# One hybrid SSM and attention layer on Trainium2: the first SSM gate tile fetched into another pool, the last query block copied out at once, one branch output fetched earlier

## The chip, the cores and the metric

The kernel runs on one core of one Trainium2 chip. Time is the device time of one execution, in microseconds (us). Three runs of the kernel before gave 1013.17, 1014.81 and 1015.25 us, a median of 1014.81. A further execution was taken under the profiler: 1013.51 us, in which the span from the first to the last instruction is 1011.5 us. The remaining 2.0 us lie around the span.

Engines go by short names: PE is TensorE (matmuls), DVE is VectorE, ACT is ScalarE, POOL is GpSimd, SP is SyncE, which here issues nearly all of the DMAs.

## The reference, cut to what matters

One layer of a streaming encoder over a prompt of 1024 tokens and a sample of 32 new tokens with 512 cached ones. The model width is 1024, there are 8 heads of 64, and everything is float32.

```
h = rms_norm(x, g_norm) * (1 + scale) + shift
z = h @ w_in              # u, zs | q, k, v, za | indexer | two merge gates g_s, g_a
ys = ssm_scan(u ...)      # S5 state space model, then gelu, GLU, * silu(zs)
o  = dsa_attend(q, k, v)  # each 64-token chunk attends to the keys the indexer picks
ya = o * silu(za)
merged = sigmoid(g_s) * (ys @ w_ps) + sigmoid(g_a) * (ya @ w_pa)
x = x + gate * (merged @ w_o)
y = rms_norm(x, g_final)
```

Outputs are y for prompt and sample, the new keys and values, the indexer keys and the SSM states.

## The kernel before

**Products.** A float32 product is made of three PE matmuls. Each operand is split into a rounded high part and the low rest (names ending in H and L, or wh and wl for a weight), and high times high, low times high and high times low are added in PSUM (`mm3`, lines L271, L272, L273). A split costs a cast on ACT (L75) and a subtraction on DVE (L78), or for weights a cast (L259 or L263) and a subtraction on POOL (L264). The 1056 tokens are handled as three blocks of 256, 384 and 416 (`BW`), so the third block holds the end of the prompt and the 32 sample tokens.

**The weight stream Z.** Nearly all products with `w_in` and `w_ps` are jobs of a list, the `Stream` object `Z`. One job is 128 output columns: 8 (or 4) steps in depth for each of the three blocks. A job's block is built in a PSUM tile `pz`, of which there are two (`ps_z`). When its last matmul has been emitted, an evacuation `ev` reads the PSUM tile and frees it. `Z` does not emit this `ev` at once: it is put on a list (`Z.after`) and comes out once a given estimate of PE time (`Z.lag`, 1.0 in the attention part, or the job's own `lag`) has been emitted beyond it. PE, DVE and ACT run in the order in which the program emits their instructions, so the lag decides in front of which other DVE and ACT work an evacuation stands.

**Attention.** The heads go in four pairs p = 0 to 3. Each pair has a key job K, a value job V and a query job Q (`Heads`, K0 to Q3). For each row block of a pair the main loop emits scores on PE into `pss`, maxima and score tiles `Sm` on DVE (L1409), a scaling (L1425), transposes on PE into `pt` (L1496), the split of the transposed probabilities into PH (ACT, L1498) and PL (DVE, L1499), the product with V on PE into `pspo` (L1513, L1515), and the output `ob` and `ya` (L1518 to L1521). Between these steps `run(us)` lets `Z` emit some of its products as filler. A pair's output `ya` goes to memory (`yaD[p]`); pair 3 is split straight into `b3H`, `b3L`. The `ev` of a query job makes two ACT copies, one for each head (`qs`, L1332), two DVE subtractions (L1336), and for the third block two small DVE copies of the sample queries (`qsm`, L1338).

**The SSM product.** After Q3 the stream holds eight jobs m0 to m7, the product of the stored SSM output with `w_ps`. When m0 begins, `switch()` closes one pool and opens `fin` and `fb`, and `ps_branch` loads the stored SSM output into 24 tiles `b`, the operand parts of m0 to m7, block by block. Tiles `m` (`m1` in the code) hold the gate of each job: `m_load(f)` loads `thD[f]`, 528 KB, from a buffer in memory, and the job's `ev` on DVE (L1612, lag 0) multiplies it with the product in place. `m_load(0)` and `m_load(1)` are issued behind the 24 loads, `m_load(f + 2)` when job f begins.

**The attention product.** When attention ends, `yaD[0]` to `yaD[2]` are loaded from memory as `src` and `srs` (L1769, L1770) and split into `b` tiles. The three splits are emitted `SA`, `SA + SB` and `SA + 2 SB` estimated microseconds of stream time later (4, 5, 6). Then come eight jobs of the product with `w_pa` into `psm`, a PSUM set of four tiles. Each block goes through `evac_a`: DVE multiplies it with the attention gate `tgl` (L1799), adds a quarter of the m tile (L1800), ACT makes the high part `mH`, DVE the low part `mL` (L78). The tiles `tgl` come from memory (`thD[8 + f]`, L1811) into tag `stg`, a pool of two tiles; the first two of them are fetched far ahead, in the attention part. The last stage multiplies the merged tiles with `w_o`.

**SP** issues DMAs in program order. A DMA whose destination tile or semaphore is not free yet holds back those behind it.

Of the kernel before, what the change touches and what calls it, by code (L numbers as in the profile page):

```python
# [7 lines left out]
F32 = mybir.dt.float32  # L8
F32R = mybir.dt.float32r
# [7 lines left out]
T, TS, D = 1024, 32, 1024  # L17
NT = T + TS
# [22 lines left out]
KA, LA = 5.0, 1.0  # L41
RE = 2.9
LAG, RS, MS, RM, RB = 4.5, 4.6, 0.008, 14.0, 1
FA, FF, SA, SB = ((1.0, 2.4), (1.1, 2.4), (1.1, 1.4), (1.5, 1.5)), 0.08, 4.0, 1.0
YR = 3.9, 2.0, 2.0, 8.0, 3.0
MR, ML, YS, YW, HI, HG, JO, SF = (), 1, 10, 15, 0, 0, 8, (2, 2, 2, 1)
C_U, C_ZS, C_Q, C_K, C_V, C_ZA, C_QI, C_KI, C_GM = 0, 512, 1024, 1536, 2048, 2560, 3072, 3584, 3656
# [16 lines left out]
def body(nc, tc, I, O, dbg=None):  # L64
# [3 lines left out]
    te, ve, se, ge, sp = nc.tensor, nc.vector, nc.scalar, nc.gpsimd, nc.sync  # L68

    def f32(ap):  # L70
        return ap.bitcast(F32)
# [10 lines left out]
    stg = ctx.enter_context(tc.tile_pool(name="stg", bufs=2))  # L82
# [226 lines left out]
    class Later:  # L309
        def __init__(self, eng, todo):  # L310
            self.eng, self.todo = eng, todo
# [159 lines left out]
    for k in range(7):  # L471
        n = 1 << k
# [208 lines left out]
    wcol = lambda c, n=128: w_in[:, c:c + n]  # L681
# [89 lines left out]
    for t in START.split():  # L771
# [6 lines left out]
        else:  # L778
            n = t.rstrip("0123456789")
# [418 lines left out]
    for k in range(9):  # L1198
        n = 128 if k < 8 else 32
# [50 lines left out]
    yaD = [dram.tile([128, NT], F32, name=f"yaD{q}") for q in range(4)]  # L1250
# [8 lines left out]
    def cp(eng):  # L1259
        return se.copy if eng is se else eng.tensor_copy  # L1260
# [45 lines left out]
    class Heads:  # L1306

        def __init__(self, p, heng, eng):
            self.eng, self.V2, self.heng_v = eng, [None, None], ve if p == 0 else ge
            self.p, self.cs = p, slice(128 * p, 128 * p + 128)  # L1310
            self.kH, self.kL, self.qs = [None, None], [None, None], [None, None]
            self.ready, self.want = False, []

            def kbegin():
                self.kf = zfp.tile([128, NT], F32, name="zf", bufs=2)
                return lambda n, ps: cp(eng)(self.kf[:, ns(n)], ps)

            def vbegin():
                self.vf = zfp.tile([128, NT], F32, name="zf", bufs=2)
                return lambda n, ps: cp(eng)(self.vf[:, ns(n)], ps)  # L1320

            def qbegin():
                self.qs = [ap_.tile([128, T], F32R, name=f"qs{e}", bufs=1 + e) for e in range(2)]
                self.qsm = ap_.tile([128, 2, TS], F32, name="qsm", bufs=2)
                ge.memset(self.qsm, 0.0)

                def ev(n, ps):
                    w = min(BW[n], T - B0[n])
                    c = slice(B0[n], B0[n] + w)
                    for e in range(2):  # L1330
                        r = slice(64 * e, 64 * e + 64)
                        se.copy(self.qs[e][r, c], ps[r, 0:w])  # L1332
                    for e in range(2):
                        r, o = slice(64 * e, 64 * e + 64), slice(64 - 64 * e, 128 - 64 * e)
                        q_ = self.qs[e]
                        ve.tensor_sub(q_[o, c], ps[r, 0:w], f32(q_[r, c]))  # L1336
                        if n == 2:
                            ve.tensor_copy(self.qsm[r, e], ps[r, w:BW[2]])  # L1338
                return ev

            job = lambda n, c0, b, end: Job(f"{n}{p}", wcol(c0 + 128 * p), b, end, heng=heng, leng=ge)
            self.kjob, self.vjob = (job("K", C_K, kbegin, lambda: self.kside()),
                                    job("V", C_V, vbegin, lambda: self.vside()))
            self.qjob = job("Q", C_Q, qbegin, None)
# [239 lines left out]
    m1, PB = [], []  # L1584

    def ps_branch():
        for h in range(2):
            PB.append({})
        for n in range(2, -1, -1):
            for q in range(4):  # L1590
                for h in range(2):
                    PB[h][q, n] = late["fb"].tile([128, BW[n]], F32R, name=f"b{h}{q}{n}")
        for n in range(3):
            for q in range(4):
                for h in range(2):
                    sp.dma_start(f32(PB[h][q, n]), ysD[h][q][:, ns(n)])
        for f in range(2):
            m_load(f)

    def m_load(f):  # L1600
        if f < 8:
            m1.append(late["fin"].tile([128, NT], F32, name="m1", tag="mm", bufs=8))
            sp.dma_start(m1[f], thD[f])

    def psjob(f):
        def begin():
            if not f:
                switch()
            m_load(f + 2)

            def ev(n, ps):
                ve.scalar_tensor_tensor(m1[f][:, ns(n)], m1[f][:, ns(n)], 1.0, ps, op0=ALU.add, op1=ALU.mult)  # L1612
            return ev
        return Job(f"m{f}", I["w_ps"].rearrange("o d e -> (o d) e")[:, 128 * f:128 * f + 128], begin, kt=4, lag=0,
                   heng=se, leng=ge, rhs=lambda n, k: (PB[0][k, n], PB[1][k, n]))
# [77 lines left out]
    seq, first, half, end = [], {}, {}, {}  # L1693
# [7 lines left out]
    late = {}  # L1701

    def switch():
        st.close()
        late["fin"] = ctx.enter_context(tc.tile_pool(name="fin", bufs=1, reuse_waits="tile"))
        late["fb"] = stB.enter_context(tc.tile_pool(name="fb", bufs=1, reuse_waits="tile"))
        ps_branch()
    stB = ExitStack()
    for k in range(len(seq) + 3):
        it = at(k)  # L1710
        if k in first:
            p, begin = first[k]
            k0 = k
            if p:
                Z.until(f"Q{p}")
            if p == 3:
                b3H, b3L = (zfp.tile([128, NT], F32R, name=n, tag="zf", bufs=2) for n in ("b3H", "b3L"))
            else:
                Z.upto(f"V{p + 1}")
            begin()  # L1720
        if it:
            e_ = max(it.e, 0) if it.e >= 0 or p == 3 else 1
        f = FA[p][e_] + FF * (it.i + 1 if it else 5)
        if not k:
            run(RE)
        if it:
            it.scores()
        if k in half and p < 3:
            HD[p + 1].want.append(0)
            HD[p + 1].heads()  # L1730
            Z.upto(f"K{p + 2}" if p < 2 else "m7")
        if p and k == k0 + 2:
            HD[p].want.append(1)
            HD[p].heads()
        if it:
            it.maxima()
        if at(k - 1):
            at(k - 1).norm(0)
        run(f * 0.4)
        Z.turns(2)  # L1740
        if at(k - 3):
            at(k - 3).out()
        if k - 3 in end and end[k - 3][0] < 3:
            end[k - 3][1]()
            HD[p].values(1)
        if k + 3 in end and p < 3:
            Z.until(f"v{p + 1}")
            HD[p + 1].values(0)
        run(f * 0.3)
        if at(k - 2):  # L1750
            at(k - 2).turn()
        if at(k - 1):
            at(k - 1).norm(1)
        if it:
            it.exps()
        run(f * 0.3)
# [4 lines left out]
    wo = ctx.enter_context(tc.tile_pool(name="wo", bufs=1, side="right", reuse_waits="tile"))  # L1761
# [2 lines left out]
    Z.load(len(Z.jobs) - 1)  # L1764
    raw_a = wload(w_pa[:, 0:128], 4, 128)
    for q in range(3):
        src = f32(wo.tile([128, 2, 512], F32R, name="src", tag=("o16", "o17", "o07")[q]).rearrange("p a b -> p (a b)"))
        sms = wo.tile([128, TS], F32, name=f"srs{q}")
        sp.dma_start(src, yaD[q][:, 0:T])  # L1769
        sp.dma_start(sms, yaD[q][:, T:NT])  # L1770
        h_, l_ = (mp.tile([128, NT], F32R, name=f"b{h}{q}", tag="b" + "0123"[2 * q + h] if q < 2 else f"b{4 + h}")
                  for h in range(2))
        aH.append(h_)
        aL.append(l_)

        def parts(h_=h_, l_=l_, src=src, sms=sms):
            split(h_[:, 0:T], l_[:, 0:T], src, se, ve)
            split(h_[:, T:NT], l_[:, T:NT], sms, se, ve)
        Z.after(SA + q * SB, parts)
# [12 lines left out]
    mL = []  # L1792
    ps_phase()
    def evac_a(f, c, tg, ps):
        if len(mL) == f:
            mL.append(late["fin"].tile([128, NT], F32R, name="mL", tag="mm", bufs=8) if f else
                      fl_.tile([128, NT], F32R, name="mL0"))
        m2 = stg.tile([128, GM], F32, name="m2", tag="sth")[:, :c.stop - c.start]
        ve.scalar_tensor_tensor(m2, tg, 1.0, ps, op0=ALU.add, op1=ALU.mult)  # L1799
        ve.scalar_tensor_tensor(m2, m1[f][:, c], 0.25, m2, op0=ALU.mult, op1=ALU.add)  # L1800
        split(mH[f][:, c], mL[f][:, c], m2, se, ve)
        if c.stop == NT:
            ge.tensor_copy(mS[:, f, 0:32], mH[f][:, T:NT])
            ge.tensor_copy(mS[:, f, 32:64], mL[f][:, T:NT])
# [72 lines left out]
    for rows in ((0, 1, 2), (8,), (3,), (4,), (5,), (6,), (LAST,)):  # L1877
        xts = {}
        for hcol in range(2):
            for i in rows:  # L1880
                n = 128 if i < 8 else 32
# [67 lines left out]
```

## Time and profile before

| | before |
|---|---|
| times of three runs | 1013.17, 1014.81, 1015.25 us |
| the profiled execution's own time | 1013.51 us |
| its span | 1011.5 us |
| DVE busy | 763.3 us (75%) |
| ACT busy | 524.6 us (52%) |
| POOL busy | 234.6 us (23%) |
| mean granted TensorE clock | 0.991 |
| DMA traffic | 124.24 MB, mean 123 GB/s |

A row of the timeline gives the start in us, the duration in us, the engine, the source line, the operation, the tiles as output<-input, the shape and the number of instructions merged into the row. What stands in brackets is the idle time of the engine ahead of the row and what ended it; `issue` is time in which the engine waited for nothing that the profile can name. SPq rows are DMA issues: the duration is that of the issue, not of the transfer. A row of the windows view gives the stretch, its length, the busy time and count of PE, PEld, DVE, ACT and POOL, the granted clock of PE (1.00 is full speed), the busy share of the DMA engines and GB/s. Matmuls are pipelined: one of 416 columns is shown 0.35 us long, while the next one starts 0.19 us after it.

### The profile page before, as it was taken

What the parts mean: (1) busy time and instruction counts of PE and PEld (TensorE: products, weight loads), DVE (VectorE), ACT (ScalarE), POOL (GpSimd) and SP (SyncE); (2) the same over time, 40 slices, a digit from 0 to 9 for tenths busy, and PEclk for the clock granted to TensorE, in tenths of its full rate; (3) what the DMA queues carried; (4) which work ended last, traced back from release to release, by engine and by line L of the source; (5) the groups of instructions that cost most, each with busy time, mean ns of one, the idle gap of its engine ahead of it and who ended that gap; (6) DMA issues with size and microseconds to landing.
All of it is one profiled execution on the core that took longest, in us unless ns stands there. A gap on an engine that the chain in (4) does not pass through costs nothing.

```text
span 1011.5 us, 16910 instructions
## 1 busy us (share of the span) xinstructions
PE 968.2 (96%) x6034; PEld 904.1 (89%) x6034; DVE 763.3 (75%) x1747; ACT 524.6 (52%) x1126; POOL 234.6 (23%) x443
## 2 busy tenths in 40 slices
PE   5999999999999999999999989999998999999997
PEld 2789999999998898999999979899897989898786
DVE  4669979994776878889999976577577785885543
ACT  3642234433555656858896365565575564443111
POOL 3202400000000024343322743233222222430000
PEclk9999999999999999999999999999999999999999
DMA  9923425437484222333323422231329403552311
GB/s 315 289 66 101 133 70 140 113 95 203 164 256 151 64 63 64 105 83 98 118 74 114 141 87 64 85 106 55 107 66 332 136 22 109 182 188 105 126 63 62
DMA packets 134400, 124.24 MB, mean 123 GB/s; under 512 B 20401, under 2 KB 115077, under 8 KB 134317
## 3 DMA queue, kind: packets, MB, share of 16 engines
q1 hardware_dynamic: 133376, 122.62, 39.3%
q8 instruction: 47, 0.77, 0.3%
q10 hardware_dynamic: 780, 0.52, 0.2%
q14 instruction: 37, 0.30, 0.1%
q0 software_dynamic: 160, 0.03, 0.0%
HBM read 87.74 MB, written 34.83 MB: 121 GB/s over the span
## 4 chain that ended last, share of the span: by engine, by line
PE 50%; DVE 14%; ACT 10%; issue 4%; DMA 1%; POOL 0%; SPq 0%; POOLq 0%; ACTq 0%; DVEq 0%
PE pz L271 8%; PE pz L272 7%; PE pz L273 7%; ACT junkb L1567 7%; PE pss L1403 3%; PE pt L1496 3%; DVE junk L1569 3%; PE psm L1918 3%; PE psm L1919 3%; PE psm L1920 3%; PE pspo L1515 2%; PE pspo L1513 2%; PE psm L272 1%; PE psm L273 1%; PE psm L271 1%
## 5 line engine op out<-in xcount | busy, mean ns | idle before, releaser
L271 PE MATMUL pz<-hH,wh 128*128 128x384 f32 (+4 forms) x744 | 254.5, 342 | 2.4 <-ACT tg L713 2.0
L272 PE MATMUL pz<-hL,wh 128*128 128x384 f32 (+4 forms) x744 | 246.2, 331 | 0.0
L273 PE MATMUL pz<-hH,wl 128*128 128x384 f32 (+4 forms) x744 | 246.0, 331 | 0.0
L264 POOL TENSOR_TENSOR wl<-raw,wh 128x256 fp32r<-128x256 f32 (+1 forms) x180 | 134.7, 776 | 126.5 <-ACT wh L259 116.0
L271 PEld LDWEIGHTS pz<-hH,wh 128*128 128x128 f32 (+1 forms) x744 | 140.4, 189 | 7.5 <-ACT tg L713 2.3
L272 PEld LDWEIGHTS pz<-hL,wh 128*128 128x128 f32 (+1 forms) x744 | 139.9, 188 | 1.8
L273 PEld LDWEIGHTS pz<-hH,wl 128*128 128x128 f32 (+1 forms) x744 | 139.6, 188 | 1.4
L1567 ACT ACTIVATE junkb<-sco,thr 128x768 bf16<-128x768 f32 (+3 forms) x128 | 96.7, 756 | 31.0 <-DVE thr L1643 20.1
L1569 DVE TENSOR_SCALAR_CACHE_REDUCE junk<-sco,thr 128x1024 bf16<-128x1024 f32 (+2 forms) x96 | 105.5, 1098 | 2.2
L271 PE MATMUL pss<-hH,wh 128*128 128x256 f32 (+2 forms) x304 | 97.6, 321 | 0.1
L272 PE MATMUL pss<-hL,wh 128*128 128x256 f32 (+2 forms) x304 | 95.7, 315 | 0.0
L273 PE MATMUL pss<-hH,wl 128*128 128x256 f32 (+2 forms) x304 | 95.4, 314 | 0.0
L263 POOL CAST wh<-raw 128x256 fp32r<-128x256 f32 x88 | 38.0, 471 | 180.9 <-PE pz L272 109.6
L1498 ACT CAST PH<-pt 128x512 fp32r<-128x512 f32 (+2 forms) x96 | 43.0, 482 | 41.5 <-PE pt L1496 37.4
L1499 DVE TENSOR_TENSOR PL<-pt,PH 128x512 fp32r<-128x512 f32 (+2 forms) x96 | 50.4, 551 | 14.6 <-ACT PH L1498 13.7
L271 PEld LDWEIGHTS pss<-hH,wh 128*128 128x128 f32 x304 | 58.6, 193 | 2.6 <-issue 1.6
L272 PEld LDWEIGHTS pss<-hL,wh 128*128 128x128 f32 x304 | 58.1, 191 | 0.3 <-DVE hL L78 0.2
L1236 DVE SCALAR_TENSOR_TENSOR sco<-rl,wi,sco 128x384 f32<-128x384 f32 (+6 forms) x49 | 46.9, 963 | 15.2 <-ACT rl L1231 14.1
L273 PEld LDWEIGHTS pss<-hH,wl 128*128 128x128 f32 x304 | 58.1, 191 | 0.0
L1231 ACT ACTIVATE rl<-pss 128x384 f32<-128x384 f32 (+6 forms) x56 | 40.9, 738 | 28.6 <-PE pss L1229 23.1
L1416 ACT ACTIVATE Sm<-Sm,mx 128x128 f32<-128x128 f32 (+8 forms) x68 | 52.7, 775 | 0.8 <-DVE mx L1409 0.8
L1920 PE MATMUL psm<-o,mL 128*128 128x512 f32 (+1 forms) x136 | 51.8, 381 | 0.0
(401 smaller groups left out, 2174.9 us busy)
## 6 DMA issues: line engine op xcount, KB each, us to landing
raw<-in_w_in SPq DMA_DIRECT2D x44, 512.0 KB
thD<-tg SPq DMA_DIRECT2D x16, 528.0 KB
wm<-in_w_mod SPq DMA_DIRECT2D x8, 1024.0 KB
tgl<-thD SPq DMA_DIRECT2D x8, 528.0 KB
m<-thD SPq DMA_DIRECT2D x8, 528.0 KB
rraw<-in_w_mod SPq DMA_DIRECT2D x4, 1024.0 KB
kd<-kd SPq DMA_DIRECT2D x32, 128.0 KB
xo<-in_x_prompt SPq DMA_DIRECT2D x8, 512.0 KB
```

Source lines behind the costliest of these rows:

```text
L264: leng.tensor_sub(wl[:, c], raw[:, c], f32(wh[:, c]))
L271: te.matmul(ps, wh, xh, start=first, stop=False)
L272: te.matmul(ps, wh, xl, start=False, stop=False)
L273: te.matmul(ps, wl, xh, start=False, stop=last)
L1231: se.activation(rl[:m, :nk].rearrange("p (b c) -> p b c", c=w_), pv, AF.Relu)
L1236: ve.scalar_tensor_tensor(sco[i][:m, :nk], rl[:m, :nk], w, sco[i][:m, :nk], op0=ALU.mult, op1=ALU.add)
L1416: se.activation(P, P, AF.Exp, scale=-1.0, bias=self.mx, accum_out=self.rs)
L1498: se.copy(PH[:, b0:b1_, oc], src)
L1499: ve.tensor_sub(PL[:, b0:b1_, oc], src, f32(PH[:, b0:b1_, oc]))
L1567: se.activation(junkb[:m, :nk], x[:m], AF.Sign, bias=t, accum_out=cnt[:m, k:k + 1])
L1569: ve.tensor_scalar(junk[:m, :nk], x[:m], t, None, op0=ALU.is_lt, op1=ALU.add, accum_out=cnt[:m, k:k + 1])
L1920: te.matmul(ps, ml, wh, start=False, stop=last)
```

## The change

Three edits, made together. Line numbers from about L1341 on are shifted by 1 to 12 in the changed kernel.

1. The job Q3 gets `lag=0`, so that each of its blocks is copied out as soon as its last matmul is emitted.
2. `m_load(0)` leaves `ps_branch` and moves to the middle of pair 2, into a tile of tag `stg`. That is the place and the tile in which the first `tgl` was fetched; the first `tgl` now goes where the second was, and the second `tgl` is fetched when a tile of the pair becomes free, in the `w_pa` stage. The `m` and `mL` tiles get fixed tags `mm0` to `mm7` in place of one tag with eight buffers.
3. `yaD[0]`, stored since the end of pair 0, is loaded as one tile `y0` of 528 KB (tag `mm7`) when job m2 begins, during pair 3. The reload of q = 0 as `src` and `srs` at the end of attention goes; its split reads `y0`. The three splits are emitted at 1.0, 3.5 and 6.0 (`SA, SB = 1.0, 2.5`).

```
-..., 4.0, 1.0
+..., 1.0, 2.5                                   # the last two are SA, SB
...
-            job = lambda n, c0, b, end: Job(f"{n}{p}", wcol(c0 + 128 * p), b, end, heng=heng, leng=ge)
+            job = lambda n, c0, b, end: Job(f"{n}{p}", wcol(c0 + 128 * p), b, end, heng=heng, leng=ge,
+                                            lag=0 if f"{n}{p}" == "Q3" else None)
...
-        for f in range(2):
-            m_load(f)
+        m_load(1)

     def m_load(f):
         if f < 8:
-            m1.append(late["fin"].tile([128, NT], F32, name="m1", tag="mm", bufs=8))
+            m1.append(late["fin"].tile([128, NT], F32, name="m1", tag=f"mm{f - 1}") if f else
+                      stg.tile([128, NT], F32, name="m1", tag="stg"))
             sp.dma_start(m1[f], thD[f])
+
+    def y0_load():
+        late["y0"] = late["fin"].tile([128, NT], F32, name="y0", tag="mm7")
+        sp.dma_start(late["y0"], yaD[0])
...
             m_load(f + 2)
+            if f == 2:
+                y0_load()
...
             Z.upto(f"K{p + 2}" if p < 2 else "m7")
+            if p == 2:
+                m_load(0)
...
     for q in range(3):
-        src = ...
-        sms = ...
-        sp.dma_start(src, yaD[q][:, 0:T])
-        sp.dma_start(sms, yaD[q][:, T:NT])
+        if q:
+            ...
+        else:
+            src, sms = late["y0"][:, 0:T], late["y0"][:, T:NT]
...
-            mL.append(late["fin"].tile([128, NT], F32R, name="mL", tag="mm", bufs=8) if f else
+            mL.append(late["fin"].tile([128, NT], F32R, name="mL", tag=f"mm{f - 2 if f > 1 else 7}") if f else
```

**DVE around the third block of Q3.** This is the program's order on DVE, in the last row blocks of pair 2. `qs_8318` and `qs_8319` (`qs_8320` and `qs_8321` in the changed kernel) are the query tiles of pair 3's two heads, `PL` the probabilities' low part, `Sm` a score tile, `m_8713` the gate tile of m0. Before:

```order
L1521 TENSOR_TENSOR ya<-ob,ya 64x256
L1499 TENSOR_TENSOR PL<-pt,PH 128x4x128
L1499 TENSOR_TENSOR PL<-pt,PH 128x128
L1409 ISA Sm,mx<-pss,mb_3324 128x512
L1409 ISA mx 128x1
L1409 ISA Sm,mx<-pss,mb_3324,mx 128x512
L1409 ISA mx 128x1
L1421 RECIPROCAL rs<-rs 128x1
L1425 TENSOR_SCALAR Sm<-Sm,rs 128x896
L1336 TENSOR_TENSOR qs_8318<-pz,qs_8318 64x384
L1338 COPY qsm<-pz 64x32
L1336 TENSOR_TENSOR qs_8319<-pz,qs_8319 64x384
```

In the changed kernel the same place reads:

```order
L1522 TENSOR_TENSOR ya<-ob,ya 64x256
L1336 TENSOR_TENSOR qs_8320<-pz,qs_8320 64x384
L1338 COPY qsm<-pz 64x32
L1336 TENSOR_TENSOR qs_8321<-pz,qs_8321 64x384
L1338 COPY qsm<-pz 64x32
L1500 TENSOR_TENSOR PL<-pt,PH 128x4x128
L1500 TENSOR_TENSOR PL<-pt,PH 128x128
L1410 ISA Sm,mx<-pss,mb_3324 128x512
```

The four instructions that read the PSUM tile `pz` of Q3's third block moved ahead of two `PL`, two score steps and the scaling. PE's own order up to the end of Q3 is the same in both.

**ACT at the end of attention.** These are the casts that make the high parts for the `w_pa` stage; the `b` with the lowest number is q = 0. `wh` is a weight cast of the `w_pa` stage. Before:

```order
L75 CAST b3H<-qs_8843 64x512
L75 CAST b_9794<-src 128x1024
L75 CAST b_9794<-srs_9791 128x32
L259 CAST wh<-raw 128x512
L75 CAST b_9800<-src 128x1024
L75 CAST b_9800<-srs_9797 128x32
L75 CAST b_9806<-src 128x1024
L75 CAST b_9806<-srs_9803 128x32
```

In the changed kernel:

```order
L75 CAST b3H<-qs_8843 64x512
L75 CAST b_9792<-y_9059 128x1024
L75 CAST b_9792<-y_9059 128x32
L75 CAST b_9798<-src 128x1024
L75 CAST b_9798<-srs_9795 128x32
L259 CAST wh<-raw 128x512
L75 CAST b_9804<-src 128x1024
L75 CAST b_9804<-srs_9801 128x32
```

The first cast reads `y0` (here `y_9059`) in place of a fresh `src`, and the weight cast moved from behind the first split to behind the second.

**SP at the same place.** These are its rows from the last weight load ahead of the reloads; what stands in brackets is what a row waits for, by the names of the semaphores: `DMAHW` for the end of an earlier DMA, else the engine. `thD_215`, `thD_216` and `thD_217` are the attention gates of f = 0, 1 and 2. Before:

```order
L250 DMA raw<-in_w_pa 128x4x128 [waits DMAHW3_49,DMAHW7_49,Activation_49,Pool_49]
L1769 DMA src<-yaD_4200 128x1024 [waits PE_49]
L1770 DMA srs_9791<-yaD_4200 128x32
L1769 DMA src<-yaD_4201 128x1024
L1770 DMA srs_9797<-yaD_4201 128x32
L1769 DMA src<-yaD_4202 128x1024 [waits DMAHW4_49]
L1770 DMA srs_9803<-yaD_4202 128x32 [waits DMAHW5_49]
```

In the changed kernel, on to the first gate load that is issued there:

```order
L250 DMA raw<-in_w_pa 128x4x128 [waits DMAHW3_49,Activation_49,Pool_49]
L1779 DMA src<-yaD_4201 128x1024 [waits DMAHW0_49,PE_49]
L1780 DMA srs_9795<-yaD_4201 128x32
L1779 DMA src<-yaD_4202 128x1024
L1780 DMA srs_9801<-yaD_4202 128x32
L1833 DMA gate_10411<-growD 128x1024 [waits DMAHW4_49]
L1833 DMA gate_10412<-growD 32x1024 [waits DMAHW5_49]
L1836 DMA gf<-in_g_final 128x1024 [waits DMAHW6_49]
L250 DMA raw<-in_w_pa 128x4x128 [waits DMAHW7_49,Activation_49,Pool_49]
L1823 DMA tgl<-thD_216 128x1056 [waits DMAHW0_49,DVE_49]
```

Two loads fewer stand there, so that q = 1 and q = 2 each move up one place, and the gate of f = 1 is loaded there, after a wait for DVE, where before the first gate load of this stretch was that of f = 2 (`thD_217`).

More of the change, by code (lines that the diff above doesn't have):

```diff
@@ L43 @@
 LAG, RS, MS, RM, RB = 4.5, 4.6, 0.008, 14.0, 1
-FA, FF, SA, SB = ((1.0, 2.4), (1.1, 2.4), (1.1, 1.4), (1.5, 1.5)), 0.08, 4.0, 1.0
+FA, FF, SA, SB = ((1.0, 2.4), (1.1, 2.4), (1.1, 1.4), (1.5, 1.5)), 0.08, 1.0, 2.5
 YR = 3.9, 2.0, 2.0, 8.0, 3.0
@@ L1766, in body @@
     for q in range(3):
-        src = f32(wo.tile([128, 2, 512], F32R, name="src", tag=("o16", "o17", "o07")[q]).rearrange("p a b -> p (a b)"))
-        sms = wo.tile([128, TS], F32, name=f"srs{q}")
-        sp.dma_start(src, yaD[q][:, 0:T])
-        sp.dma_start(sms, yaD[q][:, T:NT])
+        if q:
+            src = f32(wo.tile([128, 2, 512], F32R, name="src", tag=("", "o17", "o07")[q]).rearrange("p a b -> p (a b)"))
+            sms = wo.tile([128, TS], F32, name=f"srs{q}")
+            sp.dma_start(src, yaD[q][:, 0:T])
+            sp.dma_start(sms, yaD[q][:, T:NT])
+        else:
+            src, sms = late["y0"][:, 0:T], late["y0"][:, T:NT]
         h_, l_ = (mp.tile([128, NT], F32R, name=f"b{h}{q}", tag="b" + "0123"[2 * q + h] if q < 2 else f"b{4 + h}")
```

## The prediction

> **What bounds the kernel now.** I read the page's shares of busy time first, then PE's waits, then windows around the places that the change touches. A row of the waits view gives the idle us that ended at that instruction, how often, and the longest.
>
> ```profile
> PE 968.2 (96%) x6034; PEld 904.1 (89%) x6034; DVE 763.3 (75%) x1747; ACT 524.6 (52%) x1126; POOL 234.6 (23%) x443
> ...
> PE pz L271 <- issue: 3.8, 1, 3.8
> PE psm L271 <- ACT b L75: 1.2, 3, 0.6
> ...
> 770.00:780.00 10.00, 7.71 (x40) 6.73 (x41) 5.13 (x15) 2.44 (x6) 1.78 (x5) 0.83 1.04 404
> 856.00:868.00 12.00, 10.72 (x62) 9.34 (x61) 5.94 (x12) 4.12 (x7) 1.71 (x4) 1.00 0.88 277
> ```
>
> PE is busy 96% of the span, so a change pays only where PE idles or runs at a lower clock. The change touches two such places: one single idle of 3.8 us at 770, with the granted clock of that window down to 0.83, and short waits for the casts of `b` at 856 to 868, 1.28 us by the window (12.00 less 10.72). No PE instruction is added or removed, so everything below is waits and clock.
>
> **Edit 1, Q3 copied out at once.** These are the rows around the long idle: PE, DVE, ACT.
>
> ```profile
> 765.24 0.35 PE L273 MATMUL pz<-hH,wl 128*128 128x416 f32 x1
> 768.19 0.28 PE L273 MATMUL pz<-b,wl 128*128 128x256 f32 x1
> 772.29 0.66 PE L271 MATMUL pz<-b,wh 128*128 128x384 f32 x1 [3.82 <-issue]
> ...
> 766.07 1.16 DVE L1521 TENSOR_TENSOR ya<-ob,ya 64x256 f32<-64x256 f32 x1
> 767.26 0.89 DVE L1499 TENSOR_TENSOR PL<-pt,PH 128x512 fp32r<-128x512 f32 x2
> 770.66 0.55 DVE L1336 TENSOR_TENSOR qs<-pz,qs 64x384 fp32r<-64x384 f32 x1
> 771.23 0.18 DVE L1338 COPY qsm<-pz 64x32 f32<-64x32 f32 x1
> 771.43 0.56 DVE L1336 TENSOR_TENSOR qs<-pz,qs 64x384 fp32r<-64x384 f32 x1
> 772.00 0.20 DVE L1338 COPY qsm<-pz 64x32 f32<-64x32 f32 x1
> ...
> 765.07 0.37 ACT L1518 COPY ob<-pspo 64x256 f32<-64x256 f32 x1 [1.37 <-PE pspo L1515]
> 769.12 0.96 ACT L1332 CAST qs<-pz 64x384 fp32r<-64x384 f32 x2
> ```
>
> The profile calls the idle "issue", but the time fits a PSUM wait. `pz` has two tiles; the second block of m0 takes the one that held Q3's third block, finished by PE at 765.59. Its last reader, the second `qsm` copy, ends at 772.20, and PE starts at 772.29. In the changed order these four readers stand right behind `ya`, which ends at 767.23. ACT is free at 765.44, so its two casts (0.96) are through by about 766.6 and hold nothing up. The four take 0.55 + 0.18 + 0.56 + 0.20 = 1.49, with gaps about 1.55: the tile is free at 768.8, and PE, done with the first block at 768.47, goes on at about 768.9. Idle 0.4 in place of 3.82: **3.4 us**.
>
> The idle also costs clock. The windows below are stretches at half clock; the two PE rows are other idles.
>
> ```profile
> 771.69:775.10 3.41, 2.81 (x11) 2.74 (x12) 0.49 (x2) 0.62 (x2) 0.00 (x0) 0.50 1.06 401
> 457.66:461.07 3.41, 3.41 (x10) 3.27 (x11) 3.27 (x9) 2.65 (x7) 0.00 (x0) 0.50 0.79 235
> ...
> 457.60 0.69 PE L271 MATMUL pz<-hH,wh 128*128 128x416 f32 x1 [1.96 <-ACT tg L713]
> 716.66 1.09 PE L1496 MATMUL pt<-idf,Sm 128*128 128x128 f32 x8 [1.21 <-ACT Sm L1423]
> ```
>
> Half clock came after an idle of 1.96, not after one of 1.21, so 0.4 should not bring it. In the first window PE worked 2.81 us at half speed, which is 1.40 us of work done late: **1.4 us** more. The stretch starts on a grid of 3.41 us, so other executions may have lost 0.7 to 1.7 here. [...]
>
> What is late next? The two `PL`, the scores and the scaling now run 1.5 us later, and PE runs ahead by 4.8.
>
> ```profile
> 776.33 0.42 DVE L1612 SCALAR_TENSOR_TENSOR m<-m,pz 128x256 f32<-128x256 f32 x1 [4.13 <-DMA m<-thD]
> 778.43 0.88 PE L1515 MATMUL pspo<-PL,V 128*128 128x256 f32 x6
> 779.14 0.35 PE L271 MATMUL pz<-b,wh 128*128 128x416 f32 x1
> ...
> 770.07 0.32 SPq L1596 DMA_DIRECT2D b<-ysLD  x1
> GB/s 0 89 290 265 124 260 244 266 299 211 294 276 172 328 332 315 357 361 399 398 394 412 406 391 425 414 413 414 383 339 374 356 271 265 321 425 401 328 36 234
> ```
>
> DVE: 4.13 us before m0's first gate product went to waiting for `m`, the tile that **edit 2** now loads during pair 2; without this wait DVE has room for the 1.5. By summing durations `PL` for the products at 778.43 is ready near 773.5, and PE comes there at 778.43 − 4.8 = 773.6: no margin, so 0 to 0.5 of new wait, taken as 0. Transfers: the last `b` left at 770.07 with its seven predecessors in flight, since each DMA here waits for the end of the one eight before it. That is at most 8 x 0.21 MB = 1.7 MB, and the row of GB/s (slices of 0.875 us from 755) shows about 0.4 MB a us: estimated landings from 771.1 to 774.3. PE wants the first pair of that block at 779.14 − 4.8 = 774.3 and the last 1.7 later, so they are in time by 1.7 or more. If they weren't, at most the 3.4 and 1.4 would be cut by the lateness. The moved `m_load(0)` stands on SP where a load of the same size stood, so it costs nothing there; behind the 24 `b` loads one load fewer is queued.
>
> **Edit 3, q = 0 fetched ahead.** The rows of SP, ACT and PE at the passage from attention to the `w_pa` product:
>
> ```profile
> 855.53 0.50 SPq L1769 DMA_DIRECT2D src<-yaD  x1
> ...
> 859.75 1.05 ACT L75 CAST b<-src 128x1024 fp32r<-128x1024 f32 x1 [4.34 <-DMA src<-yaD]
> 862.93 1.05 ACT L75 CAST b<-src 128x1024 fp32r<-128x1024 f32 x1 [0.85 <-DMA src<-yaD]
> 864.64 1.05 ACT L75 CAST b<-src 128x1024 fp32r<-128x1024 f32 x1 [0.54 <-DMA src<-yaD]
> ...
> 859.91 0.35 PE L273 MATMUL pz<-b,wl 128*128 128x416 f32 x1
> 864.03 0.75 PE L271 MATMUL psm<-b,wh 128*128 128x256 f32 x3 [0.44 <-ACT b L75]
> 868.40 0.34 PE L271 MATMUL psm<-b3H,wh 128*128 128x384 f32 x1
> 874.21 0.34 PE L271 MATMUL psm<-b3H,wh 128*128 128x384 f32 x1
> ```
>
> Three loads of 0.53 MB, the first issued at 855.53, land at about 859.7, 862.9 and 864.6; PE's last earlier work ends at about 860.1 (859.91 and the 0.19 until the next could start), then it follows the casts. One job of the stage takes 874.21 − 868.40 = 5.81, so 1.45 for each q. From 860.1 to 868.40 PE does q = 0, 1, 2 of f = 0 (4.36) and the 256-token block of f = 1 (256/1056 of 5.81 = 1.41): 5.77 of work in 8.30, 2.5 lost. After: q = 0 is split by 860 from a tile that landed long before. q = 1 takes the first place in the queue and its cast ends at 860.8, before PE is through with q = 0 at 861.55. q = 2 takes the second place: cast from 862.93 to 863.98, while PE gets there at 860.1 + 2.9 + 0.24 = 863.24. It waits 0.74, and loses hardly anything elsewhere: **1.7 us** gained (bounds: 0, if q = 2 lands as late as now, and 2.5, if there is no wait). `y0` itself adds 0.53 MB to SP's queue during pair 3, a stretch in which PE's waits name no DMA. I cost it at 0, at most 0.5.
>
> **The new wait.** The second gate tile is now loaded only when f = 0's gate tile is free, as the third is now:
>
> ```profile
> 870.09 0.59 DVE L1799 SCALAR_TENSOR_TENSOR m<-tgl,psm 128x416 f32<-128x416 f32 x1
> 871.84 0.41 DVE L1799 SCALAR_TENSOR_TENSOR m<-tgl,psm 128x256 f32<-128x256 f32 x1
> ...
> 870.70 0.33 SPq L1811 DMA_DIRECT2D tgl<-thD  x1
> 893.50 0.38 SPq L1835 DMA_DIRECT2D rawo<-in_w_o  x1
> ...
> 896.77 1.14 ACT L75 CAST o<-rawo 128x512 fp32r<-128x512 f32 x2 [0.94 <-DMA rawo<-in_w_o]
> ...
> 868.00:880.00 12.00, 12.00 (x76) 11.90 (x75) 11.60 (x25) 5.32 (x11) 6.21 (x14) 1.00 0.43 137
> 880.00:908.00 28.00, 28.00 (x172) 27.70 (x171) 24.69 (x46) 11.28 (x22) 12.64 (x25) 1.00 0.51 172
> ```
>
> Issued at 870.70 − 1.7 = 869.0, it lands 3.3 later, as the 512 KB load issued at 893.50 and used at 896.77: 872.3 (4.2, as `src` at 855.53, gives 873.2). f = 1's first gate product, now at 871.84 and so due at 870.1, waits 2.2 for it on DVE, with every later gate product and `mL` queued behind it, and frees its PSUM tile at 872.7. PE needs that tile, the fourth in turn, for the second block of f = 2, at 874.21 − 1.7 = 872.5. Cost **0.3** (0 to 1.2). Afterwards DVE is 2.2 behind. Its spare share is 3.31 in 28 by the last window, 0.69 in a job of 5.81, so it catches up within some 19 us, three jobs, in which PE's four tiles are just enough.
>
> **Sum.** 3.4 + 1.4 + 1.7 − 0.3 = 6.2 us. The profiled execution, 1013.51 with its span of 1011.5, becomes 1007.3; the median of the runs, 1014.81, would become 1008.6. I take the mean of all four executions, 1014.2, less 6.2: **1008.0**.
>
> **Rivals.**
> - *Fast transfers:* q = 2 lands early and the new gate too. If q = 2 is there by 862.2, 0.7 before the second landing of now, its cast ends before PE's 863.24. Gain 3.4 + 1.4 + 2.5 = 7.3: 1006.9. For it: the queue is shorter. Against: the landings above lie 1.7 to 3.2 apart. [...]
> - *Transfers bound both ends:* q = 2 lands where it does now and the gate load takes 4.2. Gain 4.8 + 0 − 1.2 = 3.6: 1010.6. For it: in 856 to 868 the DMA engines are 88% busy.
> - *DVE takes the long idle's place:* `PL` and the scores pushed back run longer than before, as `ya` did at 766.07 (1.16 for a 64x256 that reads no PSUM), and PE waits about 1.5 at the products of 778.43, with half clock again (1.4). Gain 6.2 − 2.9 = 3.3: 1010.9. For it: no margin. If edit 1 frees the tile late after all, the result is near this too.
> - *Slower:* the wait for the gate feeds itself. Each gate load starts when DVE frees a tile, so a DVE that stays late loads the next gate late, and waits again. It decides if DVE's spare 0.69 a job does not shrink the 2.2: DVE's 24.69/28 of 5.81, 5.12 a job, would have to rise to 5.81. Then PE loses 2.2 − 0.7 = 1.5 in each of the seven jobs left, 10.5 in place of 0.3: 6.5 − 10.5 = 4.0 slower, 1018.2. Against: the 12% spare, and from f = 2 on a tile that has long been free.
>
> **How the numbers follow.** Forecast 0.62, fast transfers 0.10, slow transfers 0.14, DVE in PE's way 0.09, slower 0.05. The range reaches from the fast case with a phase of the clock grid that gives 1.7 (gain 7.6) and 1.5 us of scatter, as the three runs have, to the slow cases and 0.6 more: 1005.2 to 1011.5. A measurement here tells about 0.2% from no change, 2 us; only the DVE rival's worse half, with part of edit 3 lost as well, ends within that. Faster 0.62 + 0.10 + 0.14 + 0.04 = 0.90, same 0.05, slower 0.05.
>
> **What would show it.** Edit 1: no idle above 0.6 before m0's second block, clock 1.00 from 770 to 780, and the `m` gate product with no DMA wait. Edit 3: the first cast at the passage with no DMA wait and q = 2's cast ending near 863.98 less 4.8. New wait: DVE idle some 2 us at the first gate product of f = 1, PE under 1. Wrong would be: a new PE wait of over 1 us for `PL`, for `b` or for `psm`.

## The result and the profile after

Four runs of each kernel, among them the three shown before: 1007.57 us median (1005.85 to 1008.86) against 1014.65 (1013.17 to 1015.25). The ratio is 0.9934 with a 95% interval of 0.9916 to 0.9951, so about 7 us faster, within 5 to 8.5. The profiled execution of the changed kernel took 1005.85 us. The ratios below leave out one slow execution, of no_q3: 1069.14 us at a granted clock of 0.845.

The page of the changed kernel, PE's waits from 750 us on, and two windows (the columns are those of the windows above):

```profile
span 1003.9 us, 16913 instructions
...
PE 961.5 (96%) x6034; PEld 898.6 (90%) x6034; DVE 763.8 (76%) x1747; ACT 525.2 (52%) x1126; POOL 234.3 (23%) x443
...
PE pz L271 <- PE pz L273: 0.7, 1, 0.7
PE psm L273 <- POOL wl L264: 0.7, 1, 0.7
...
770.00:780.00 10.00, 10.00 (x69) 9.57 (x69) 8.78 (x25) 6.26 (x13) 0.56 (x3) 1.00 1.04 394
851.00:863.00 12.00, 11.35 (x71) 10.98 (x70) 7.86 (x16) 4.21 (x8) 4.94 (x8) 1.00 0.64 205
```

The idle of 3.8 has become 0.7, the window from 770 has full clock and PE busy throughout. At the passage to the `w_pa` product PE no longer waits for `b`; it waits once for POOL.

To see where the time went, PE's rows are lined up at four landmarks that both kernels have: the first matmul of m0, the last matmul of m7, the second block of f = 1 and the second block of f = 2 in the `w_pa` stage. The first line is of the kernel before (its others stand above: 859.91, 868.40, 874.21), the four behind it are of the changed kernel:

```profile
765.89 0.37 PE L271 MATMUL pz<-b,wh 128*128 128x256 f32 x1
...
763.64 0.37 PE L271 MATMUL pz<-b,wh 128*128 128x256 f32 x1
...
853.46 0.35 PE L273 MATMUL pz<-b,wl 128*128 128x416 f32 x1
...
860.32 0.34 PE L271 MATMUL psm<-b3H,wh 128*128 128x384 f32 x1
...
866.36 0.44 PE L271 MATMUL psm<-b3H,wh 128*128 128x384 f32 x1
```

Differences of these starts, and the rest up to the end of the span, for the two kernels and in the same way for every kernel of the experiments:

| profile | up to m0 | m0 to the end of m7 | passage | f = 1 to f = 2 | rest |
|---|---|---|---|---|---|
| before | 765.89 | 94.02 | 8.49 | 5.81 | 137.3 |
| changed | 763.64 | 89.82 | 6.86 | 6.04 | 137.5 |
| changed, second profile | 765.16 | 89.80 | 6.99 | 6.00 | 137.5 |
| changed, third profile | 766.94 | 89.80 | 5.95 | 6.21 | 137.6 |
| q3_only | 764.95 | 94.56 | 7.91 | 5.81 | 137.3 |
| gate_only | 764.83 | 94.26 | 8.70 | 6.02 | 137.4 |
| no_q3 | 763.97 | 94.29 | 7.45 | 6.09 | 137.5 |
| q3_gate | 766.36 | 89.85 | 8.69 | 5.98 | 137.4 |
| q3_gate_again | 766.88 | 89.81 | 8.48 | 6.22 | 137.4 |
| sasb_old | 765.20 | 89.85 | 6.96 | 6.18 | 137.5 |
| qsm_act | 765.41 | 90.71 | 7.17 | 6.14 | 137.6 |
| wl3_first | 765.48 | 89.81 | 6.04 | 6.05 | 137.5 |
| wl3_again | 766.50 | 89.80 | 6.68 | 6.02 | 137.5 |

The span fell by 7.6. Of this 2.25 arose before m0, a part in which PE's order is the same and which differs by up to 3.3 us between these profiles, in no order that follows the edits. What the change did is in the other columns: −4.20, −1.63, +0.23 and about +0.2, together 5.4.

### The profile page after: what moved, and what is told of

Read it like the earlier page. It is cut to its first block, busy times and chain, and to the rows that moved or that the text cites. A ratio compares the mean times of both kernels' runs of the same rounds, so it can differ in the third digit from the quotient of the medians.

```text
span 1003.9 us, 16913 instructions
## 1 busy us (share of the span) xinstructions
PE 961.5 (96%) x6034; PEld 898.6 (90%) x6034; DVE 763.8 (76%) x1747; ACT 525.2 (52%) x1126; POOL 234.3 (23%) x443
```

## The experiments

Each kernel is the one before or the changed one with one edit. Where ratios are given, they are to the kernel before, timed in the same job on the same chip.

### Each edit without the others

**q3_only** adds to the kernel before only:

```
+                                            lag=0 if f"{n}{p}" == "Q3" else None)
```

> Edit 1 alone (Q3 copied out at once), the gate tile of m0 and all else as before. My theory: edit 1 needs edit 2. The idle of 3.8 before m0's second block shrinks to about 0.7, but DVE then stands at m0's first gate product until the tile m lands (776.3 in the profile before) with six PL queued behind it, so PE idles about 4 us at the product pspo<-PL, and half clock follows again. Net 0.8 us faster than before (0 to 1.5). Rival A (the edits are independent): 4.2 us faster, as in the changed kernel, with no new wait of PE.

Ratio 1.0003 (0.9989 to 1.0016): nothing gained. PE's timeline, and DVE's m0 gate product and the `PL` behind it, with a window:

```profile
768.26 0.41 PE L271 MATMUL pz<-b,wh 128*128 128x384 f32 x1 [0.73 <-PE pz L273]
776.29 1.37 PE L1516 MATMUL pspo<-PL,V 128*128 128x256 f32 x6 [2.87 <-DVE PL L1500]
...
775.21 0.42 DVE L1613 SCALAR_TENSOR_TENSOR m<-m,pz 128x256 f32<-128x256 f32 x1 [3.83 <-DMA m<-thD]
775.55 1.01 DVE L1500 TENSOR_TENSOR PL<-pt,PH 128x512 fp32r<-128x512 f32 x2
...
773.00:778.00 5.00, 2.13 (x12) 1.91 (x11) 2.64 (x9) 0.31 (x1) 0.41 (x2) 0.86 1.03 412
```

The idle before m0's second block falls to 0.73, as in the changed kernel. But DVE then stands for 3.83 us at the gate product, for the tile `m` that is still behind 24 loads, and PE meets the missing `PL` 8 us later, idles 2.87 and gets a lowered clock again. The wait was moved, not removed; m0 to m7 takes 94.56 where it took 94.02. This is the order of events that my theory gave, with an idle of 2.87 where it had about 4; its gain of 0.8 us does not show in the times, and the rival of independent edits falls.

**gate_only** takes edit 2 alone:

```
-        for f in range(2):
-            m_load(f)
+        m_load(1)
...
+            if p == 2:
+                m_load(0)
```

> Edit 2 alone (gate tile of m0 loaded during pair 2, second gate of the w_pa stage loaded late), Q3 and the reload of q = 0 as before. My theory: the idle of 3.8 stays, since PE waits there for the qsm copies of Q3 and not for the gate; half clock stays; the late second gate costs 0.2. Time 0.2 slower than before (0.3 faster to 0.5 slower). Rival B (the idle named issue was the wait for m, which the profile shows on DVE for 4.13 us): the idle goes and the kernel is about 4 us faster.

Ratio 1.0004 (0.9992 to 1.0016). PE's wait, and DVE's gate product:

```profile
771.23 0.66 PE L271 MATMUL pz<-b,wh 128*128 128x384 f32 x1 [3.82 <-issue]
...
770.93 0.19 DVE L1338 COPY qsm<-pz 64x32 f32<-64x32 f32 x1
771.16 0.42 DVE L1612 SCALAR_TENSOR_TENSOR m<-m,pz 128x256 f32<-128x256 f32 x1
```

DVE finds its `m` ready and no longer waits, yet the idle of 3.82 stays to the hundredth, and it ends 0.11 after the second `qsm` copy (770.93 and 0.19). So "issue" hid the wait for Q3's PSUM tile, and rival B falls. The late second gate shows too: 6.02 in place of 5.81.

**q3_gate** joins the two, without edit 3; q = 0 is loaded as `src` and `srs` and the splits come at 4, 5 and 6, as before:

```
+                                            lag=0 if f"{n}{p}" == "Q3" else None)
...
+            if p == 2:
+                m_load(0)
```

> Edits 1 and 2 without edit 3 (q = 0 loaded at the end as before, splits at 4, 5, 6). My theory: the idle of 3.8 falls to 0.7 with full clock, 4.2 gained; the waits for the casts of b at the passage stay as before; 0.2 lost at the second gate: 4.0 us faster than before (3.3 to 4.7). Rival C (part of the gain at 770 comes from the changed load queue of edit 3): under 3 us faster.

> Edits 1 and 2 without edit 3: 4.0 us faster than before (0.996). Rival: as fast as the changed kernel.

Ratios 0.9949 (0.9933 to 0.9964) and 0.9957 (0.9943 to 0.9972), 4.8 us by the mean of the two, where 4.0 (3.3 to 4.7) was expected. By the trace m0 to m7 takes 89.85 and 89.81, as in the changed kernel, and the passage 8.69 and 8.48, as long as before. The joint gain at 770 is all there without edit 3; rival C falls.

**no_q3** is the changed kernel without edit 1:

```
-                                            lag=0 if f"{n}{p}" == "Q3" else None)
+            job = lambda n, c0, b, end: Job(f"{n}{p}", wcol(c0 + 128 * p), b, end, heng=heng, leng=ge)
```

> Edits 2 and 3 without edit 1. My theory: the idle of 3.8 and the half clock stay, PE's passage to the w_pa product gains 1.6 and the second gate costs 0.2: 1.4 us faster than before (0.9 to 2.0). Rival B: about 5.4 faster, since the gate was the cause. Rival D (nothing at the passage, the rest is scatter): no difference.

Ratio 1.0000 (0.9987 to 1.0013). The idle of 3.82 is back, as my theory has it. The 1.4 us did not show in the times: their interval reaches down to 1.3 us faster. In the trace the passage takes 7.45, 1.04 less than before, and the late gate costs 0.28 of that. Rival B falls. Rival D, nothing at the passage, is not excluded by this time: beside gate_only, the same kernel without edit 3, it gives 0.4 us. That edit 3 gains something is shown by the passages alone, 5.95 to 7.45 in the six profiles with it (old order of POOL's pieces) and 7.91 to 8.70 in the five without.

### The changed kernel again, and what bounds the passage

> The changed kernel once more, beside the variants below. My theory (edit 1 with edit 2 about 4.2, edit 3 about 1.2 after the POOL wait that shows at the passage, less 0.2): 5.2 us faster than before, 0.9949 as a ratio; the first comparison's 7.1 contained scatter. Rival (the 7.1 is right): 0.993.

> The changed kernel: 5.2 us faster than before (0.995), 1.2 faster than without edit 3 by the traces. Rival: edit 3 gives nothing, the two agree.

Ratios 0.9962 (0.9945 to 0.9979) and 0.9953 (0.9935 to 0.9971). With the first comparison's 0.9934 the mean is 0.9950, 5.1 us, which agrees with the 5.4 of the landmarks. The first comparison's 0.9934 lies just below both later intervals: some of its 7 us was most likely scatter, and the rival of 0.993 is not borne out. Against the kernel without edit 3 on the same chip the third comparison gives 0.9953 to 0.9957, again 0.4 us, where the traces have 1.2. The sign is right, but the rival that edit 3 gives nothing lies within the intervals.

The new end of the passage shows in these rows of the changed kernel (SP, ACT, DVE, PE, POOL); the last is POOL's same step in the kernel before:

```profile
849.12 0.46 SPq L1779 DMA_DIRECT2D src<-yaD  x1
...
853.15 1.05 ACT L75 CAST b<-src 128x1024 fp32r<-128x1024 f32 x1 [3.01 <-DMA src<-yaD]
...
854.23 0.62 ACT L259 CAST wh<-raw 128x512 fp32r<-128x512 f32 x1
855.14 1.05 ACT L75 CAST b<-src 128x1024 fp32r<-128x1024 f32 x1 [0.30 <-DMA src<-yaD]
...
856.25 1.46 DVE L78 TENSOR_TENSOR b<-src,b 128x1024 fp32r<-128x1024 f32 x1
...
858.08 0.39 PE L273 MATMUL psm<-b3H,wl 128*128 128x256 f32 x1 [0.65 <-POOL wl L264]
...
854.93 3.10 POOL L264 TENSOR_TENSOR wl<-raw,wh 128x128 fp32r<-128x128 f32 x4 [6.30 <-ACT wh L259]
...
862.15 1.71 POOL L264 TENSOR_TENSOR wl<-raw,wh 128x128 fp32r<-128x128 f32 x4 [7.08 <-ACT wh L259]
```

The load of q = 2 is there 2.0 us after that of q = 1 (its cast starts at 855.14) and PE does not wait for it. What PE waits for is POOL's low part of f = 1's weight. It starts only after ACT's weight cast, which stands behind the cast of the first reload in both kernels (q = 1 here, q = 0 before), and takes 3.10 where it took 1.71, beside DVE's subtractions, the second of which takes 1.46 where the three of the kernel before take 1.22 to 1.23. In gate_only and q3_gate, without edit 3, the four pieces meet the same subtractions and take 3.09 too; PE waits 0.82 (gate_only) and 0.8 (q3_gate) for them there, on top of 0.85 and 0.9 for the cast of `b`. So edit 3 took away the wait for the cast and did not create the one for POOL.

**wl3_first** makes POOL's four pieces in the order in which PE uses them:

```
-        for a in range(0, kt, pc):
+        for a in order or range(0, kt, pc):
...
-        wh, wl = wparts(raw_a, 4, 128)
+        wh, wl = wparts(raw_a, 4, 128, order=(3, 0, 1, 2))
```

> The changed kernel, with the four POOL subtractions for each w_pa weight made in the order in which PE uses them (3, 0, 1, 2 instead of 0, 1, 2, 3). My theory: what ends last at the passage is POOL's low part of f = 1, not a load; PE's wait of 0.65 for wl goes, the b3H 384 of f = 1 comes 0.7 us earlier against the end of m7's last block, and nothing else moves: 0.7 us faster than the changed kernel (0.3 to 0.9), visible in the trace and too small for the times. Rival (q = 2's load or DVE's subtractions stand right behind it): the wait moves to PE's matmul on b of q = 2 and the passage stays as long.

> The variant with POOL's pieces in PE's order once more, beside the changed kernel and the one without edit 3 on one chip. My theory: 0.8 us faster than the changed kernel, 6.0 faster than before (ratio 0.994). Rival: no difference to the changed kernel.

Ratios 0.9931 (0.9913 to 0.9949) and 0.9944 (0.9925 to 0.9962), each the lowest of its job, where the changed kernel had 0.9962 and 0.9953; the intervals overlap. PE's and POOL's rows, first of wl3_first, then PE's of wl3_again and POOL's of the changed kernel's third profile:

```profile
857.65 0.39 PE L273 MATMUL psm<-b3H,wl 128*128 128x256 f32 x1
...
856.73 3.10 POOL L264 TENSOR_TENSOR wl<-raw,wh 128x128 fp32r<-128x128 f32 x4 [6.28 <-ACT wh L259]
...
859.31 0.38 PE L273 MATMUL psm<-b3H,wl 128*128 128x256 f32 x1 [0.43 <-POOL wl L264]
...
857.89 2.13 POOL L264 TENSOR_TENSOR wl<-raw,wh 128x128 fp32r<-128x128 f32 x4 [5.98 <-ACT wh L259]
```

The first wl3 profile has no wait, though POOL takes the same 3.10, and a passage of 6.04. The second waits 0.43 and takes 6.68, because q = 1 landed late, and with it ACT's weight cast. Compared at the same landing (the first `src` cast 4.7 us after its issue, in wl3_again as in no_q3) the passage is 6.68 against 7.45; at 4.0 (wl3_first, changed kernel) it is 6.04 against 6.86. So by these pairs of single profiles the order is worth 0.8. But in the changed kernel's third profile the first load was there after 3.7 us and that of q = 2 only 2.4 us behind it. DVE's second subtraction began only 1.73 after POOL's pieces (859.62, 857.89), these took 2.13, nothing waited and the passage took 5.95. That POOL's low part ended last in five of the six profiles with edit 3 and the old order is shown; that it does so each time is not so.

**sasb_old** puts `SA, SB` back to 4.0, 1.0 in the changed kernel:

```
-FA, FF, SA, SB = ..., 1.0, 2.5
+FA, FF, SA, SB = ..., 4.0, 1.0
```

> The changed kernel with SA, SB back at 4.0 and 1.0. PE's and ACT's order stay, DVE takes m7's gate products ahead of the subtractions of q = 0 and q = 1. My theory: the gain at the passage comes from the early load, not from the spacing: within 0.3 us of the changed kernel, the same waits of PE. Rival (the spacing makes it): PE waits for DVE's low part of q = 0 or 1, 0.5 to 1.5 us slower.

Ratio 0.9958 (0.9940 to 0.9976); passage 6.96, and PE waits 0.76 for `wl` and for no `b`. The gain at the passage comes from the early load, not from the spacing.

### The rest of the idle

**qsm_act** moves the two small copies of pair 3's Q job from DVE to ACT:

```
-                            ve.tensor_copy(self.qsm[r, e], ps[r, w:BW[2]])
+                            (se.copy if p == 3 else ve.tensor_copy)(self.qsm[r, e], ps[r, w:BW[2]])
```

> The changed kernel with the two qsm copies of Q3 on ACT instead of DVE. My theory: the idle of 0.72 left before m0's second block is the rest of the same wait, for DVE's last reader of Q3's PSUM tile, so it falls by the 0.38 us of the two copies to about 0.35, with full clock: 0.4 us faster than the changed kernel in the trace, too small for the times. Rival (the idle is something PE itself needs, a weight load or its pipeline, as the named releaser PE says): it stays at 0.7.

Ratio 0.9943 (0.9924 to 0.9961). The trace says no gain; ACT, DVE and PE:

```profile
767.69 0.18 ACT L1338 COPY qsm<-pz 64x32 f32<-64x32 f32 x1 [1.59 <-DVE qs L1336]
768.49 0.18 ACT L1338 COPY qsm<-pz 64x32 f32<-64x32 f32 x1 [0.62 <-DVE qs L1336]
...
767.90 0.56 DVE L1336 TENSOR_TENSOR qs<-pz,qs 64x384 fp32r<-64x384 f32 x1 [0.24 <-ACT qsm L1338]
...
768.72 0.44 PE L271 MATMUL pz<-b,wh 128*128 128x384 f32 x1 [0.74 <-ACT qsm L1338]
770.33 0.87 PE L1497 MATMUL pt<-idf,Sm 128*128 128x128 f32 x6 [0.82 <-ACT Sm L1424]
```

My size was wrong: the four readers of the PSUM tile still go one after the other, now by turns on two engines, each waiting for the other, so the last one ends no sooner. Why they don't overlap is not settled. ACT's own work slips and PE gets a second wait of 0.82 (m0 to m7: 90.71). The rival's number came true, since the idle stays at 0.74. Its reason does not fit: PE starts 0.05 after the last `qsm` copy here, as it starts 0.09 after it in both the kernel before and the changed one and 0.11 in gate_only, whether the idle is 0.72 or 3.82. And the releaser is now named: PE waits for the last reader of Q3's tile.

## Why the prediction was right, step by step

- **Edit 1, 3.4 + 1.4.** Right in its mechanism, 4.2 in place of 4.8: 3.1 from the idle and, as the difference, 1.1 from the clock. The same matmuls show that 1.1: from m0's second block to the first sample scores PE took 3.20 before (772.29 to 775.49) and takes 2.08 here (766.93 to 769.01). Of the 0.3 that is missing from the 1.4, 0.17 is a gap of PE ahead of the transposes at 767.70, where before, at half clock, there was none. The idle that is left is 0.72 and not 0.4, above the 0.6 that was named as a sign, since DVE came to `ya` 0.48 after m0's first matmul, where before it came 0.18 after it, and so the tile was free 0.3 later than worked out. The first row is of the kernel before, the others are of the changed kernel:

```profile
775.49 1.13 PE L1403 MATMUL pss<-kall,qsm 128*64 128x272 f32 x4
...
764.12 1.17 DVE L1522 TENSOR_TENSOR ya<-ob,ya 64x256 f32<-64x256 f32 x1
...
766.64 0.20 DVE L1338 COPY qsm<-pz 64x32 f32<-64x32 f32 x1
...
766.93 0.42 PE L271 MATMUL pz<-b,wh 128*128 128x384 f32 x1 [0.72 <-PE pz L273]
...
769.01 1.13 PE L1404 MATMUL pss<-kall,qsm 128*64 128x272 f32 x4
...
763.71 1.30 POOL L78 TENSOR_TENSOR kL<-kd,kH 128x512 fp32r<-128x512 f32 x1 [0.67 <-DVE kH L77]
```

  `ya` takes 1.17 here, where POOL's `kL` runs beside it (from 763.71, 1.30); the median of the 24 `ya` of this shape is 0.42. The sum carried this 1.16 from the row before, rightly.
- **"4.13 us went to waiting for `m`".** Right, and it weighs more than the text gave it: it was used as room for 1.5 us of DVE work, while q3_only shows that without edit 2 nothing at all is left of the 4.2. Neither edit is worth anything alone.
- **"No margin" for `PL`, taken as 0.** Right: PE has no wait there in the changed kernel, and 2.87 in q3_only.
- **Edit 3, 1.7.** The size was right, 1.63 here and 1.55 as the difference of the means with and without it (6.90 of the six profiles that have it and the old order of POOL's pieces, 8.45 of five), but the step "q = 2 waits 0.74" was not: q = 2 came early, as the fast rival had it, and POOL's low part, which the working did not look at, took a wait of about the same length (0.65). That the size came out is therefore luck: one wait that was counted and did not come was replaced by one that was not counted. Without either the gain would have been the 2.5 of that rival: a passage of 5.95 was seen once. The times give 0.4 us in two comparisons and are too coarse to tell 0 from what the traces show.
- **The new wait, 0.3.** 0.23 here, 0.17 to 0.41 over the profiles with edit 2. The load took what was worked out, but DVE waited 0.85 for it and not 2.2. The working had f = 1's first gate product next in DVE's order; the `mL` of f = 0's last block now stands ahead of it, where before it stood behind:

```profile
862.62 0.33 SPq L1823 DMA_DIRECT2D tgl<-thD  x1
...
864.44 0.59 DVE L78 TENSOR_TENSOR mL<-m,mH 128x416 fp32r<-128x416 f32 x1 [0.61 <-ACT mH L75]
865.88 0.99 DVE L1811 SCALAR_TENSOR_TENSOR m<-tgl,psm 128x256 f32<-128x256 f32 x2 [0.85 <-DMA tgl<-thD]
```

  "PE's four tiles are just enough" missed about 0.2 in the rest of the stage (137.3 to 137.5). The slower rival, a wait that feeds itself, did not come.
- **The sum.** 6.2 forecast, 5.4 by the landmarks and 5.1 by three comparisons; so the forecast was about 1 us too high in its gain, mostly in the clock and the idle left of edit 1. That the forecast time of 1008.0 met 1007.57 still more closely is luck: in the profiled execution 2.25 us ahead of m0 came on top. By its own terms (1014.2 − 7.6 − 1.5) the range began at 1005.1 and not at 1005.2, which changes nothing.

## What to carry to other kernels

An idle that the profile calls "issue" is worth looking up by hand: here the last reader of the buffer that the next instruction overwrites ended 0.09 us before it (before) and 0.11 (gate_only). When a wait goes, follow the same engine's queue to its next wait before counting the gain: here one edit freed a tile, the other removed the next stop 8 us on, and each alone gave nothing. At a passage between stages, check every producer of the first matmul, the weight's low part on POOL as well as the loads, and try making pieces in the order in which they are used.

## What the runs showed of the hardware

- POOL's four pieces of `wl` and DVE's `b` subtractions took longer beside each other. The pieces took 1.71 with no `b` subtraction beside them (before, from 862.15), 2.13 beside parts of them (third profile of the changed kernel, from 857.89) and 3.10 beside both pairs (changed, from 854.93). DVE's `b` subtraction went from 1.23 (before, 864.01) to 1.46 (changed, 856.25) and its 32-column one from 0.18 (before, 861.97) to 0.45 (changed, 855.38); the one at 854.24 in the changed kernel, with POOL beside it for its last 0.53, still took 1.22, and one with POOL beside it for its first 0.40 took 1.49 (third profile, 859.62). How the length follows from the overlap is not shown.
- PE's granted clock was 1.00 around the idle of 0.72 (changed, 765 to 770), that of 0.85 (gate_only, 856 to 868) and that of 1.21 (before, 700 to 720). It was 0.50 behind the idle of 1.96 (before, 457.66 to 461.07) and 0.86 in the window that holds the idle of 2.87 (q3_only, 773 to 778). In the kernel before, half clock came after less than 1.96 too:

```profile
345.02:348.44 3.41, 3.41 (x13) 3.41 (x12) 3.20 (x4) 1.22 (x2) 0.00 (x0) 0.50 0.32 96
...
343.58 0.31 PE L1228 MATMUL pss<-kiH,qis 128*32 128x272 f32 x1 [1.48 <-ACT rl L1231]
```

  An idle of 1.48 and one of 0.23 lay in the 3.41 us ahead of that stretch, in which PE was busy for 1.70. The stretches at half clock shown here start at 345.02, 457.66 and 771.69, which are 33 and 92 times 3.413 apart. Whether the longest idle or the busy time decides is not tested here.
- The first reload of `src` was used 3.7 to 4.7 us after its issue in different profiles. In the six with edit 3 and the old order of POOL's pieces the passage took 5.95 at 3.7 and 7.45 at 4.7. A load of 528 KB (`tgl`), with a weight load issued 0.8 us behind it, was used after 3.26 (changed, 862.62 to 865.88).
